# Expert weights loaded ahead into four buffers of split weights, and the pair of experts with two blocks worked on as ninth of sixteen

## The chip, the cores and the metric

The kernel runs on one core of a Trainium2 chip. The metric is the device time of one execution, in microseconds (us); of several runs the median counts. PE is the matrix engine (TensorE), DVE the vector engine, ACT the scalar engine, POOL the general engine (GpSimd), SP the engine that here does nothing but issue transfers (DMAs).

## The reference

Two blocks follow one another on 512 tokens of width 1024: first four mixers with a gate and a dense feed-forward, then a depth of two layers, each with a mixer and a mixture of experts (MoE). The change is in the MoE, which is computed like this, cut to what matters:

```python
def hierarchical_moe(h, ...):          # 4 groups x 8 experts, top 2 of the chosen group
    g = argmax(xf @ w_group + b_group)
    vals, loc = top_k((xf @ w_expert + b_expert)[group g], 2)
    gates = pg * softmax(vals); eid = g * 8 + loc
    # tokens are gathered into blocks, each of one expert
    def expert_block(args):
        xb, e = args
        hb = silu(xb @ w_gate[e]) * (xb @ w_up[e])      # 1024 -> 512
        return hb @ w_down[e]                           # 512 -> 1024
    # weighted by the gate and added up for each token
```

An expert has three float32 matrices of 2 MiB. All 32 are loaded in each layer: 201 MB.

## The kernel before

**Pairs and blocks.** `moe` takes the experts two at a time, in 16 pairs. A block is 128 rows of tokens: the first rows belong to one expert of the pair, the others to its partner. Experts are ranked by their number of tokens, and pair u joins rank u with rank 31 - u; the four experts of pairs 0 and 1 are fixed (`STAT`), so their weights can be loaded before the ranks are known. A pair of rank 2 (`NST`) up to 2 + `MORE`, which is pair 2 alone, has a second block with rows of its heavier expert only, so that more than one block's worth of its tokens finds room. `work` lists the blocks of each pair, `flat` all blocks in order; `fetch` gathers the rows of a block by an indirect transfer on POOL's queue, two blocks ahead.

**Order of the work.** The loop over `u` in `moe` runs `gate_up` of a pair, the transposes of the next pair's rows (`next_x`), then `down` and the scatter of the pair before. In `gate_up` a step `get()` takes two pieces, one for each expert of the pair, and multiplies them with every block of the pair; `down` does likewise. A pair so takes 12 pieces: four of gate, four of up, four of down. `items_moe` writes the pieces down in that order, with each pair's down behind the next pair's gate and up: piece 0 to 7 are gate and up of pair 0, 8 to 15 of pair 1, 16 to 19 the down of pair 0, 20 to 27 gate and up of the third pair, and so on to 191.

**The stream of weights.** `Stream` hands out all weights of the kernel in the order of use. It has a ring of raw buffers (`rs`, tiles `sr`, 8 KiB in each of 128 partitions) and a ring of buffers for weights that are split into a high and a low part (`hs`, tiles `sh`, each with a half `h` and a half `l` of 4 KiB). The dense stages and the mixers use the split weights; the experts read the raw ones. During an expert stage the raw ring has 13 buffers (3 + 2 from the start, 7 and 1 added for the stage) and the split ring, which has four, is not used. `prefetch` at the head of `moe` loads pieces 0 to 12 into the ring and two more into the tiles `eys` and `lngb`, which are needed for other things only later. `raw_get` then issues further loads as far ahead as there are ring buffers: a load waits on SP's queue until PE has read the piece that its buffer held. A tile named `sr_7` appears as `sr` in the trace.

```python
            r = pool.tile([P, 2048], F32, name=tag)[:, :k * c].rearrange("p (k c) -> p k c", k=k)
            self.e.Q.dma_start(r, src() if callable(src) else src)
...
        st.prefetch([(sp, "eys"), (gb, "lngb")], e.moe_first[l])
...
            self.load(max(self.nr + n, self.nr + len(self.rs) + len(self.ahead)))
```

The matmul before the stage is the mixer's output product in `token_mm` (tile `pz`), whose last rows use all four split buffers up to its end. Between it and the experts lie the layer norm, the routing on DVE (tables `eid`, `tix`) and the first gathers (`xg`). SP reads the ranked experts' numbers into registers in `ranked` (line 2334).

Of the kernel before, what the change touches and what calls it, by code (L numbers as in the profile page):

```python
# [8 lines left out]
F32 = mybir.dt.float32  # L9
# [8 lines left out]
P = 128  # L18
# [16 lines left out]
NP = NE // 2  # L35
DE = 512
ALPHA = 4.0 ** 0.25
CAP = 128
FAR = 1000.0
STAT = ((0, 8), (1, 9))  # L40
NST = len(STAT)
WIDE = 8
MORE = 1
NB = (NP + MORE + 1) // 2 * 2
CT = 32
GPC = ((640, 448, 640, 384, 448), (832, 832, 512, 320))
# [85 lines left out]
class Stream:  # L132
# [46 lines left out]

    def load(self, n, slot=None):  # L180
        while self.nl < min(n, len(self.items) if self.last is None else self.last):
            src, k, c, _, _ = self.items[self.nl]
            self.cut(self.nl, 0)
            if slot is None:
                pool, tag = self.rs[0]
                self.rs.rotate(-1)
            else:
                pool, tag = slot
                self.ahead.add(self.nl)
            r = pool.tile([P, 2048], F32, name=tag)[:, :k * c].rearrange("p (k c) -> p k c", k=k)  # L190
            self.e.Q.dma_start(r, src() if callable(src) else src)
            self.raw[self.nl] = r
            self.nl += 1

    def split(self, n):
# [50 lines left out]
    def get(self):  # L246
        n = self.i + len(self.hs)
        self.split(n if self.limit is None else max(self.i + 1, min(n, self.limit)))
        self.i += 1
        return self.hl.pop(self.i - 1)  # L250
# [1368 lines left out]
def lru(e):  # L1619
# [159 lines left out]
    for j in range(0, KT, 2):  # L1779
        for n in (1, 2, 0):  # L1780
            st.cols(w_in, n * D + j * P)
    e.mark2 = items_token(e, I["sc_w_out_2"][0], KT)
    items_moe(e, 1)
    with tc.tile_pool(name="lo", bufs=1, reuse_waits="tile") as op:
        left = mix_ln(e, op, state["z"], [slice(0, 2)] + [slice(2 + t * P, 2 + (t + 1) * P) for t in range(NT)],
# [30 lines left out]
def expert_items(weight):  # L1816


    def half(i, k, c):
        def src(q):  # L1820
            return lambda: weight(i).rearrange("(p k) c -> p k c", p=P)[:, q * k:(q + 1) * k, :]
        return [(src(q), k, c, "k", 0) for q in range(2)]
    return half(0, 4, DE) + half(1, 4, DE) + half(2, 2, D)


def chosen(e, l, ev):

    rows = (D, D, DE)
    w = [e.I[n][l].rearrange("x k c -> (x k) c") for n in MOE_W]
    return lambda i: w[i][bass.ds(ev() * rows[i], rows[i]), :]  # L1830


def items_moe(e, l):


    def own(x):
        return lambda i: e.I[MOE_W[i]][l][x]

    def ranked(r):
        return chosen(e, l, lambda: e.ranked(r))  # L1840

    e.moe_first[l] = len(e.st.items)
    last = []
    for u in range(NP):
        pair = [own(x) for x in STAT[u]] if u < NST else [ranked(u), ranked(NE - 1 - u)]
        it = [p_ for pp in zip(*(expert_items(w) for w in pair)) for p_ in pp]
        n = len(it) * 2 // 3
        for i in it[:n] + last:
            e.st.add(*i)
        last = it[n:]  # L1850
    for i in last:
        e.st.add(*i)
# [72 lines left out]
class Moe:  # L1925
# [90 lines left out]
    def run(self):  # L2016
        moe(self.e, self)
        self.ctx.close()


def moe(e, mo):
    l, hm, nt, n_tok, dh, dy, lg = mo.l, mo.hm, mo.nt, mo.n_tok, mo.dh, mo.dy, mo.lg
    nc, tc, I, st = e.nc, e.tc, e.I, e.st
# [7 lines left out]
    gb = gbp.__enter__()  # L2031
    with ExitStack() as ph:
        sp = ph.enter_context(tc.tile_pool(name=f"mo{l}", bufs=1, reuse_waits="tile"))
        st.prefetch([(sp, "eys"), (gb, "lngb")], e.moe_first[l])
        xg = [sp.tile([P, D], F32, name=f"xg{i}") for i in range(2)]
        for x_ in xg:
            G.memset(x_, 0.0)
        def small(name, shape, dt=F32):
            return sp.tile([P] + list(shape), dt, name=name)
# [54 lines left out]
        q, r = small("cq", [2, nt]), small("cr", [2, nt])  # L2094
        so4 = big(2 * nt * NE).rearrange("p (k t c) -> p k t c", k=2, t=nt)
        for o, src in ((q, pr3[:, :nt].unsqueeze(1)), (r, rank.unsqueeze(1).unsqueeze(1))):
            V.tensor_tensor(so4, sel, src.to_broadcast([P, 2, nt, NE]), op=OP.mult)
            V.tensor_reduce(o, so4, axis=AX.X, op=OP.add)
        h, u_, w, x_, z, m1 = [small(f"c{i}", [2, nt]) for i in range(6)]
# [4 lines left out]
        stt(w, u_, float(NST + WIDE), x_, OP.is_lt, OP.mult)  # L2104
        stt(x_, r, float(NST + MORE), x_, OP.is_lt, OP.mult)
        rk = small("rk", [2, nt])
# [21 lines left out]

        sv = small("sv", [2, nt, NB], F32R)
        vk = mo.val.rearrange("p t k -> p k t")  # L2130
        V.tensor_tensor(so4[:, :, :, :NB], mo.io[:, :NB].unsqueeze(1).unsqueeze(1).to_broadcast([P, 2, nt, NB]),
                        u_.unsqueeze(3).to_broadcast([P, 2, nt, NB]), op=OP.is_equal)
        mul(sv, so4[:, :, :, :NB], vk.unsqueeze(3).to_broadcast([P, 2, nt, NB]))

        def one_hots(slot_):

            for k in range(2):
                ro = sp.tile([P, KT, P], F32R, name="ext", bufs=2)
                ro = ro[:, :nt, :]
                V.tensor_tensor(ro, slot_.unsqueeze(1).to_broadcast([P, nt, P]),  # L2140
                                rk[:, k, :].unsqueeze(2).to_broadcast([P, nt, P]), op=OP.is_equal)
                yield from ((k, i, ro[:, i, :]) for i in range(nt))

        ptab = bank("ptab")[:, :NB]
        for i_, (k, t, ro) in enumerate(one_hots(mo.slot)):
            mm(ptab, ro, sv[:, k, t, :], i_ == 0, i_ == 2 * nt - 1)
        yix = small("yix", [NB], I32)
        V.tensor_scalar(yix, ptab, -1.0, None, op0=OP.add)
# [9 lines left out]
        def xpose(i):  # L2158
            x_ = sp.tile([P, KT, P], F32, name="ext", bufs=2)
            for k0 in (0, 4):  # L2160
                pt = bank("pex")
                for k in range(4):
                    tr(pt[:, k * P:(k + 1) * P], xg[i].rearrange("p (c k) -> p k c", k=KT)[:, k0 + k, :])
                (A.copy if k0 else V.tensor_copy)(x_[:, k0:k0 + 4, :].rearrange("p k c -> p (k c)"), pt)  # L2164
            return x_
# [3 lines left out]
        def tiled(o, x_, ww, cut, start, stop):  # L2169

            for c in range(0, P, CT) if cut < P else (0,):
                w_ = CT if cut < P else P
                mm(o[c:c + w_, :], x_[:, c:c + w_], ww[c >= cut], start, stop)

        def gate_up(blocks, get):

            pp = [[bank("peg") for _ in blocks] for _ in range(2)]
            for w in range(2):
                for q in range(2):
                    ww = get()  # L2180
                    for p_, (x_, cut) in zip(pp[w], blocks):
                        for k in range(4):
                            tiled(p_, x_[:, q * 4 + k, :], [i[:, k, :] for i in ww], cut, q + k == 0, q == 1 and k == 3)
            res = []
            for (_, cut), pg, pu in zip(blocks, *pp):
                sg = sp.tile([P, DE], F32, name="eh", bufs=3)
                A.activation(sg, pg, AF.Silu)  # L2187
                mul(sg, sg, pu)
                res.append((sg, cut))
            return res  # L2190
# [9 lines left out]
        def down(blocks, get):  # L2200
            pp = [[bank("pey0"), bank("pey1")] for _ in blocks]
            for q in range(2):
                ww = get()
                for po, (h_, cut) in zip(pp, blocks):
                    for k in range(2):
                        for h in range(2):
                            tiled(po[h], h_[:, q * 2 + k, :], [w[:, k, h * 512:h * 512 + 512] for w in ww], cut,
                                  q + k == 0, q + k == 2)
            return pp

# [11 lines left out]
        def gates():  # L2222
# [28 lines left out]
            stt(b2, bs, float(NST + WIDE), b1, OP.is_lt, OP.mult)  # L2251
            stt(b1, rank, float(NST + MORE), b1, OP.is_lt, OP.mult)
            ts(bs, rank, float(NP), -2.0, OP.is_ge, OP.mult)
# [55 lines left out]
        lst = small("lst", [NL + 1], I32)  # L2309
        nov = small("nov", [1], I32)  # L2310

        work = [[u] + ([NP + u - NST] if NST <= u < NST + MORE else []) for u in range(NP)]
        flat = [b_ for bs in work for b_ in bs]

        def fetch(i):
            if i < len(flat):
                gather(i % 2, tix[:, flat[i]:flat[i] + 1])
# [23 lines left out]
        def next_x(u):  # L2341

            xs = []
            for b_ in work[u]:
                i = done[0]
                done[0] += 1
                xs.append((xpose(i % 2), P if b_ >= NP else CAP * 3 // 4 if NST <= u < NST + WIDE else CAP // 2))
                fetch(i + 2)
            return xs

        xs = next_x(0)
        gates()
        st.nr = e.moe_first[l]
# [7 lines left out]
        for u in range(NP):  # L2361
            sg = gate_up(xs, get)
            if u + 1 < NP:
                xs = next_x(u + 1)
# [5 lines left out]
            if u == NP - 2:  # L2370
                next(rows)
            hs = [(hpose(x_), cut) for x_, cut in sg]
        scatters(NP - 1, down(hs, get))
        with tc.issue_after(e.late.ins):
            for h, n in rows_:
# [109 lines left out]
```

## Time and profile before

| | us |
|---|---|
| median of 3 runs | 2599.82 (2596.87 to 2601.62) |
| the profiled execution | 2602.1 |
| its span, first to last instruction | 2600.1 |
| PE busy | 2309.3 (89%) |
| DVE busy | 939.5 (36%) |
| ACT busy | 667.3 (26%) |
| POOL busy | 239.3 (9%) |
| expert matmuls of gate and up, busy (PE L286, `peg`) | 534.5 |
| expert matmuls of down, busy (PE L286, `pey`) | 309.8 |
| mean granted TensorE clock | 0.958 |

The span of a profile begins with the first instruction; the profiled execution's own time is 2.0 us longer. Times in the rows below are us from the start of the span, times of single instructions in the page's groups are ns. "Busy" adds up the time in which at least one instruction of the group runs; the expert matmuls run four at a time beside each other. Line 286 is a helper that issues every matmul, line 191 the one that issues every load of weights, so groups are told apart by their tiles. The layer numbers are 0 and 1; layer 0's expert stage runs from about 1290 to 1778, layer 1's from about 2062 to 2550.

### The profile page before, as it was taken

The page shows a single profiled execution, that of the slowest core. Times are in us where ns is not written, and L with a number is a line of the kernel's source. Part 1 is how long each engine was busy: PE and PEld are TensorE (multiplying, and loading weights), DVE is VectorE, ACT ScalarE, POOL GpSimd, SP SyncE. Part 2 cuts the span into 40 slices and gives each one's busy share as a digit, 9 for nine tenths or more (in the row PEclk, how much of TensorE's full clock was granted, in tenths as well). Part 3 has the DMA queues.
Part 4 walks back from the last instruction along what each step waited for, and adds up shares of the span by engine and source line. Part 5 has one row for each costly group of instructions (what it writes and reads, how often), then busy time and mean ns, then how long its engine had stood idle before and what let it go on. Part 6 is the DMA issues. An engine that isn't in the chain of part 4 may idle for free. (4 is left out here: it accounts for less than half of the span.)

```text
span 2600.1 us, 37405 instructions
## 1 busy us (share of the span) xinstructions
PE 2309.3 (89%) x15293; PEld 1479.3 (57%) x15293; DVE 939.5 (36%) x2127; ACT 667.3 (26%) x1062; POOL 239.3 (9%) x268
## 2 busy tenths in 40 slices
PE   7998999999999999999699888883999699888881
PEld 6886778887888888896433222221997433222220
DVE  4348877754533322665510000004544410000003
ACT  4335332123422222584201000004322101000002
POOL 0013130000100000101200000002101110000002
PEclk9999999999999999999699999996999699999996
DMA  4221221035133333224299999996236299999993
GB/s 140 90 84 37 86 69 62 22 98 182 58 97 97 97 115 113 76 75 185 99 407 416 420 419 415 412 418 245 68 98 236 114 403 418 418 419 413 414 407 123
DMA packets 175218, 556.85 MB, mean 214 GB/s; under 512 B 22088, under 2 KB 104742, under 8 KB 124866
## 3 DMA queue, kind: packets, MB, share of 16 engines
q1 hardware_dynamic: 153156, 523.29, 52.0%
q0 software_dynamic: 12768, 25.31, 2.7%
q10 hardware_dynamic: 9120, 5.83, 0.8%
q8 instruction: 122, 2.00, 0.3%
q14 instruction: 52, 0.43, 0.0%
HBM read 548.00 MB, written 25.21 MB: 220 GB/s over the span
## 5 line engine op out<-in xcount | busy, mean ns | idle before, releaser
L286 PE MATMUL peg<-sr,ext 128*32 128x512 f32 (+1 forms) x4096 | 534.5, 595 | 90.8 <-DMA sr<-in_moe_w_gate_dram 55.4
L286 PEld LDWEIGHTS peg<-sr,ext 128*32 128x32 f32 (+1 forms) x4096 | 143.5, 110 | 426.6 <-issue 261.0
L286 PE MATMUL pey<-sr,eh 128*32 128x512 f32 (+1 forms) x2080 | 309.8, 597 | 13.9 <-DMA sr<-in_moe_w_down_dram 11.3
L286 PEld LDWEIGHTS pey<-sr,eh 128*32 128x32 f32 (+1 forms) x2080 | 84.5, 110 | 200.0 <-issue 154.2
L2164 DVE COPY ext<-pex 128x512 f32<-128x512 f32 x34 | 23.5, 690 | 407.7 <-PE pex L305 407.5
L213 DVE TENSOR_TENSOR sh_0l<-sr,sh_0h 128x1024 fp32r<-128x1024 f32 x84 | 103.5, 1232 | 162.2 <-ACT sh_0h L211 161.5
L2218 ACT COPY eys<-pey 128x512 f32<-128x512 f32 x68 | 39.9, 586 | 456.2 <-PE pey L286 455.6
L271 DVE TENSOR_TENSOR eh<-eh,peg 128x512 f32<-128x512 f32 x34 | 23.4, 688 | 349.8 <-PE peg L286 349.8
L211 ACT CAST sh_0h<-sr 128x1024 fp32r<-128x1024 f32 x84 | 88.1, 1049 | 235.9 <-PE pf L286 53.2
L213 DVE TENSOR_TENSOR sh_1l<-sr,sh_1h 128x1024 fp32r<-128x1024 f32 (+1 forms) x65 | 77.4, 1191 | 111.6 <-ACT sh_1h L211 111.3
L213 DVE TENSOR_TENSOR sh_2l<-sr,sh_2h 128x1024 fp32r<-128x1024 f32 (+1 forms) x65 | 74.4, 1144 | 95.5 <-ACT sh_2h L211 95.1
L211 ACT CAST sh_1h<-sr 128x1024 fp32r<-128x1024 f32 (+1 forms) x65 | 66.5, 1023 | 153.1 <-PE pf L286 48.5
L211 ACT CAST sh_2h<-sr 128x1024 fp32r<-128x1024 f32 (+1 forms) x65 | 62.9, 967 | 152.6 <-PE pf L286 49.3
L2187 ACT ACTIVATE eh<-peg 128x512 f32<-128x512 f32 x34 | 20.3, 597 | 288.7 <-PE peg L286 288.7
L286 PE MATMUL pl<-hlo,sh_0h 128*128 128x264 f32 (+3 forms) x288 | 87.6, 304 | 2.0 <-DVE hlo L295 2.0
L286 PE MATMUL pl<-hhi,sh_0h 128*128 128x264 f32 (+3 forms) x288 | 88.0, 305 | 0.8 <-ACT hhi L294 0.8
L2219 POOL DMA_INDIRECT dy<-eys,yix x34 | 33.8, 993 | 583.8 <-ACT eys L2218 567.4
L286 PE MATMUL pl<-hhi,sh_0l 128*128 128x264 f32 (+3 forms) x288 | 87.2, 303 | 0.0
L2154 POOL DMA_INDIRECT xg<-dh,tix x34 | 34.9, 1028 | 360.2 <-PE pex L305 299.1
L2197 DVE COPY eh<-pex 128x512 f32<-128x512 f32 x34 | 23.3, 691 | 111.8 <-PE pex L305 111.8
L2164 ACT COPY ext<-pex 128x512 f32<-128x512 f32 x34 | 19.9, 586 | 154.9 <-PE pex L305 115.9
L286 PEld LDWEIGHTS pl<-hlo,sh_0h 128*128 128x128 f32 x288 | 56.4, 196 | 4.5 <-DVE hlo L295 2.7
(714 smaller groups left out, 4881.2 us busy)
## 6 DMA issues: line engine op xcount, KB each, us to landing
sr<-in_moe_w_gate_dram SPq DMA_DIRECT2D x128, 1024.0 KB
sr<-in_moe_w_down_dram SPq DMA_DIRECT2D x128, 1024.0 KB
sr<-in_moe_w_up_dram SPq DMA_DIRECT2D x124, 1024.0 KB
sr<-in_w_in_dram SPq DMA_DIRECT2D x34, 1024.0 KB
sr<-in_sc_w_in_dram SPq DMA_DIRECT2D x12, 1024.0 KB
sr<-in_ffn_w_gate_dram SPq DMA_DIRECT2D x11, 1024.0 KB
sr<-in_ffn_w_up_dram SPq DMA_DIRECT2D x11, 1024.0 KB
sr<-in_ffn_w_down_dram SPq DMA_DIRECT2D x10, 1024.0 KB
```

The lines of the kernel that those rows point to most:

```text
L211: self.e.A.copy(hi, r)
L213: v.tensor_tensor(lo, r, f(hi), op=OP.subtract)
L271: V.tensor_tensor(out_, a, b, op=OP.mult)
L286: T.matmul(o, l, r, start=start, stop=stop)
L2154: G.indirect_dma_start(out=xg[i], out_offset=None, in_=dh[:, :], in_offset=bass.IndirectOffsetOnAxis(ap=ti, axis=0), bounds_check=n_tok - ...
L2164: (A.copy if k0 else V.tensor_copy)(x_[:, k0:k0 + 4, :].rearrange("p k c -> p (k c)"), pt)
L2187: A.activation(sg, pg, AF.Silu)
L2197: V.tensor_copy(hh.rearrange("p k c -> p (k c)"), pt)
L2218: e.late = A.copy(ys[:, h * 512:(h + 1) * 512], po[h])
L2219: G.indirect_dma_start(out=dy[:, :], out_offset=bass.IndirectOffsetOnAxis(ap=yi, axis=0), in_=ys, in_offset=None, bounds_check=2 * n_tok - ...
```

## The change

`prefetch` is also given the four split buffers (`*st.hs`), so that four more pieces (15 to 18) are loaded ahead. A split buffer is two tiles of half a piece, so such a piece comes in two transfers; a raw piece is therefore kept as a list of its 128-partition slices, and `gate_up` and `down` index that list. `ORDER` takes pair 2 out of its place and puts it in the middle: 0, 1, 3, 4, 5, 6, 7, 8, 2, 9, ..., 15. `items_moe` (the order of the loads) and `work` (that of the blocks) follow it. The number of rows of the first expert in a block (`cut`) is now chosen by the block and not by the place of the pair.

```diff
+ORDER = [u for u in range(NP) if not NST <= u < NST + MORE]
+ORDER[NP // 2:NP // 2] = range(NST, NST + MORE)
...
     def load(self, n, slot=None):
...
-            r = pool.tile([P, 2048], F32, name=tag)[:, :k * c].rearrange("p (k c) -> p k c", k=k)
-            self.e.Q.dma_start(r, src() if callable(src) else src)
-            self.raw[self.nl] = r
+            src = src() if callable(src) else src
+            if (pool, tag) in self.hs:
+
+                rr = [pool.tile([P, 1024], F32, name=tag + x).rearrange("p (k c) -> p k c", c=c) for x in "hl"]
+                for i, r in enumerate(rr):
+                    self.e.Q.dma_start(r, src[:, i * k // 2:(i + 1) * k // 2, :])
+            else:
+                rr = [pool.tile([P, 2048], F32, name=tag)[:, :k * c].rearrange("p (k c) -> p k c", k=k)]
+                self.e.Q.dma_start(rr[0], src)
+
+            self.raw[self.nl] = rr[0] if parts else [r[:, i, :] for r in rr for i in range(r.shape[1])]
...
-    for u in range(NP):
+    for u in ORDER:
         pair = [own(x) for x in STAT[u]] if u < NST else [ranked(u), ranked(NE - 1 - u)]
...
-        st.prefetch([(sp, "eys"), (gb, "lngb")], e.moe_first[l])
+        st.prefetch([(sp, "eys"), (gb, "lngb"), *st.hs], e.moe_first[l])
...
-                            tiled(p_, x_[:, q * 4 + k, :], [i[:, k, :] for i in ww], cut, q + k == 0, q == 1 and k == 3)
+                            tiled(p_, x_[:, q * 4 + k, :], [i[k] for i in ww], cut, q + k == 0, q == 1 and k == 3)
...
-                            tiled(po[h], h_[:, q * 2 + k, :], [w[:, k, h * 512:h * 512 + 512] for w in ww], cut,
+                            tiled(po[h], h_[:, q * 2 + k, :], [w[k][:, h * 512:h * 512 + 512] for w in ww], cut,
...
-        work = [[u] + ([NP + u - NST] if NST <= u < NST + MORE else []) for u in range(NP)]
+        work = [[u] + ([NP + u - NST] if NST <= u < NST + MORE else []) for u in ORDER]
...
-                xs.append((xpose(i % 2), P if b_ >= NP else CAP * 3 // 4 if NST <= u < NST + WIDE else CAP // 2))
+                xs.append((xpose(i % 2), P if b_ >= NP else CAP * 3 // 4 if NST <= b_ < NST + WIDE else CAP // 2))
```

## Rows read from the trace of the kernel before

**Rows 1.** The page, the span in 40 slices of 65 us: what the transfers moved.

```profile
GB/s 140 90 84 37 86 69 62 22 98 182 58 97 97 97 115 113 76 75 185 99 407 416 420 419 415 412 418 245 68 98 236 114 403 418 418 419 413 414 407 123
```

**Rows 2.** Waits of PE, 1280 to 1780: us in total, times, longest.

```profile
PE peg L286 <- DMA sr<-in_moe_w_gate_dram: 28.0, 18, 1.8
PE peg L286 <- DMA sr<-in_moe_w_up_dram: 17.5, 20, 1.5
...
PE pey L286 <- DMA sr<-in_moe_w_down_dram: 5.7, 11, 0.6
```

**Rows 3.** Windows of 20 us, layer 0: busy by engine, clock, DMA share, GB/s.

```profile
1240.00:1260.00 20.00, 17.34 (x113) 15.94 (x112) 9.50 (x24) 6.14 (x13) 8.32 (x8) 0.71 0.50 195
1260.00:1280.00 20.00, 5.66 (x28) 4.96 (x26) 14.88 (x78) 4.07 (x7) 1.95 (x4) 0.50 0.07 27
...
1300.00:1320.00 20.00, 20.00 (x186) 7.00 (x182) 1.98 (x3) 1.78 (x3) 1.00 (x1) 1.00 1.01 421
...
1340.00:1360.00 20.00, 20.00 (x117) 6.59 (x110) 0.69 (x1) 1.20 (x2) 0.00 (x0) 1.00 1.00 410
1360.00:1380.00 20.00, 20.00 (x176) 7.36 (x178) 2.58 (x4) 2.36 (x4) 2.05 (x2) 1.00 0.97 379
```

**Rows 4.** Timeline of SP's queue, layer 0: start, us, what it issues.

```profile
1240.79 0.42 SPq L191 DMA_DIRECT2D eys<-in_moe_w_up_dram  x1
1297.25 0.33 SPq L191 DMA_DIRECT2D sr<-in_moe_w_up_dram  x1
...
1492.38 7.96 SPq L191 DMA_DIRECT2D sr<-in_moe_w_gate_dram  x4
...
1524.66 7.97 SPq L191 DMA_DIRECT2D sr<-in_moe_w_gate_dram  x4
```

**Rows 5.** Timeline of PE, layer 0: start, us, matmuls merged by tile.

```profile
1240.22 0.40 PE L286 MATMUL pz<-sh_0h,zl 128*128 128x512 f32 x1
...
1332.64 28.88 PE L286 MATMUL peg<-sr,ext 128*32 128x512 f32 x160
...
1362.32 7.07 PE L286 MATMUL pey<-sr,eh 128*32 128x512 f32 x64
...
1370.48 13.94 PE L286 MATMUL peg<-sr,ext 128*32 128x512 f32 x128
...
1385.45 14.47 PE L286 MATMUL pey<-sr,eh 128*32 128x512 f32 x80
```

**Rows 6.** Timeline of POOL, and SP's longest single wait, layer 0.

```profile
1285.39 1.12 POOL L2154 DMA_INDIRECT xg<-dh,tix  x1 [23.45 <-DVE tix L2150]
...
1333.00 1.03 POOL L2219 DMA_INDIRECT dy<-eys,yix  x1 [5.67 <-ACT eys L2218]
...
SPq L2334 <- DVE eid L2329: 44.7, 1, 44.7
```

**Rows 7.** A window of 3 us at the first release of a buffer, layer 0.

```profile
1296.00:1299.00 3.00, 3.00 (x32) 0.91 (x28) 0.00 (x0) 0.00 (x0) 0.00 (x0) 1.00 0.32 52
```

**Rows 8.** Timeline of SP's queue, single issues behind the first pair's down.

```profile
1332.06 0.33 SPq L191 DMA_DIRECT2D sr<-in_moe_w_down_dram  x1
...
1339.94 0.34 SPq L191 DMA_DIRECT2D sr<-in_moe_w_gate_dram  x1
```

**Rows 9.** Layer 1: SP's first load after the start, POOL's first gather.

```profile
2068.74 0.33 SPq L191 DMA_DIRECT2D sr<-in_moe_w_up_dram  x1
...
2056.06 1.10 POOL L2154 DMA_INDIRECT xg<-dh,tix  x1 [28.74 <-DVE tix L2150]
```

**Rows 10.** Timelines of ACT (end of two pairs' gate, last copy) and PE (first wait).

```profile
1407.49 0.60 ACT L2187 ACTIVATE eh<-peg 128x512 f32<-128x512 f32 x1 [6.89 <-PE peg L286]
1432.92 0.60 ACT L2187 ACTIVATE eh<-peg 128x512 f32<-128x512 f32 x1 [6.23 <-PE peg L286]
...
1777.50 0.59 ACT L2218 COPY eys<-pey 128x512 f32<-128x512 f32 x1 [0.28 <-PEq L2379]
...
1446.35 2.76 PE L286 MATMUL pey<-sr,eh 128*32 128x512 f32 x18 [0.20 <-DMA sr<-in_moe_w_down_dram]
```

More of the change, by code (lines that the diff above doesn't have):

```diff
@@ L181, in load @@
         while self.nl < min(n, len(self.items) if self.last is None else self.last):
-            src, k, c, _, _ = self.items[self.nl]
+            src, k, c, _, parts = self.items[self.nl]
             self.cut(self.nl, 0)
```

## The prediction

> **What bounds the kernel now.** I read the page's 40 slices first [rows 1]. They show two stretches, slices 21 to 27 and 33 to 39, in which the transfers run at 400 to 420 GB/s: the two expert stages, one for each layer. Everything the change touches lies in them and in the slices just ahead. Next I asked whom PE waits for in layer 0's stage [rows 2]: 28.0 + 17.5 + 5.7 = 51 us, all of it for expert weights. So the stage's end is set by the last weights to land, and PE has slack. The third view, windows of 20 us, says when [rows 3]: from 1300 on the transfers are at 421 GB/s, but for a dip in 1340 to 1380, with 410 and 379. Ahead of the stage they are nearly idle: 27 GB/s in 1260 to 1280. That idle time is what the change can use.
>
> The SP queue shows why it is idle [rows 4]: the last load ahead goes out at 1240.8, and the next at 1297.25, when PE has used up its first two pieces. In between no buffer is free in the plan: 13 ring buffers and two borrowed ones (`eys`, `lngb`) hold pieces 0 to 14. Layer 1 does the same 771.5 us later [rows 9].
>
> **Four more pieces.** A piece is 1.049 MB (1024 KB); at 418.5 GB/s, between the slices' 412 to 420 [rows 1] and the window's 421 [rows 3], it takes 2.506 us. In steady state one pair of experts (12 pieces, with its gathers and scatters) takes 32.28 us, from the gate loads at 1492.38 to those at 1524.66 [rows 4]. Pieces 15 to 18 now go into the four buffers of split weights. The last matmul that reads those is at 1240.22 [rows 5], so their loads go out right behind the two borrowed ones, some 1241 to 1250. The transfers already queued end about 1250 (3.9 MB went in 1240 to 1260 [rows 3]); four pieces end about 1260. The first gather, which needs the transfers, is issued at 1285.39 [rows 6]: 25 us of cover in layer 0, and in layer 1 about 2030 against 2056.06 [rows 9]. If that cover were gone, the 10 us would stand in front of the gather and be lost again. What is left to load from 1297 on is 173 pieces in place of 177: **-4 x 2.506 = -10.0 us per layer**.
>
> The rate can be questioned. The slices give 412 to 420 GB/s over hundreds of us [rows 1], so 2.506 us it is. The Trainium skill ("HBM Reference", Specifications) puts a core's share of its memory at about 358 GB/s, and about 425 for a core that streams alone; by the share, which no window here agrees with, eight pieces would cost 23.4 us instead of 20.1, and the time would be an estimated 2576.8.
>
> The eight half loads cost SP eight issues of 0.42 us at most [rows 4], 3 us in all. Behind them SP has only the register loads of line 2334, for which it waits 44.7 us for `eid` [rows 6]; they are hidden by that, and a release as late as 1280 would still be. The larger number of views of a piece in `gate_up` and `down` issues nothing, and the cut of a block goes by its own number, so each block has its old instructions.
>
> **The queue at the hand-over.** The borrowed buffers are used once, so piece 32 must wait for the ring slot of piece 19. Pieces 19 to 31 take the slots of 0 to 12, which came free at the times of the trace. The load issued at 1297.25 moves bytes from about 1298.7 on: the window 1296 to 1299 has 52 GB/s [rows 7], which is 156 KB or 0.4 us at the full rate. So 1.4 us pass from issue to bytes. Thirteen pieces end at 1298.7 + 13 x 2.506 = 1331.3. Piece 19 is used up with the second half of the first pair's down, whose release the SP queue has at 1332.06 [rows 8]; 32 flows from 1333.5: 2.2 us empty. It ends at 1336.0. Pieces 33 and 34 wait for the first quarter of the third pair's gate and up, which with one block takes 13.94 / 4 = 3.5 us from 1332.64 on [rows 5]: out at 1336.1, flowing at 1337.5: 1.5 us empty. After that two slots come free per 3.5 us and two pieces take 5.0, so the queue fills up. Sum 3.7 us, less a scatter (0.52 MB, 1.25 us) that is issued at 1333.00 [rows 6] and has to be moved anyway: **+2.45 us** (bounds 0, if gathers fill it, and 3.7).
>
> **The pair with two blocks, moved.** Pair 2 holds two blocks: its gate and up take 28.88 us against 13.94 of the next pair, its down 14.47 against 7.07 [rows 5]; with transposes it is some 24 us longer. As third pair it holds slots while the loads could run: quarters of 7.2 us, and the queue runs empty, which is the dip of 1340 to 1380: (8.5 + 39.5) x 20 / 418.5 = 2.3 us. With the old order and four more pieces, slots come free at 1339.94 [rows 8] and every 28.88 / 4 = 7.2 us after it, and the same counting (a slot's release + 1.4 us, less the end of what is queued) gives empty times of 2.2 + 5.3 + 2.2 + 2.3 + 2.2 = 14 us: the pieces would be worth nothing. At the ninth place the queue can't run empty: PE, which does an ordinary pair in 25.4 us (the activations at 1407.49 and 1432.92 [rows 10]) against 32.28 of the loads, has by then used up its lead. In the pair's 49.4 us the loads gain 17.1 us, 6.4 pieces of the ring's 13, and some five are still to be loaded. **-2.3 us.** The 24 us by which PE then lags come back at 32.28 - 25.4 = 6.9 us a pair, in 3.5 pairs; seven follow. POOL's gathers keep their places in the row of blocks, two ahead; their number is the same.
>
> **Sum.** Per layer -10.0 + 2.45 - 2.3 = -9.8 us (bounds -12.3 and -8.6, by the bounds of the empty time); two layers -19.7 us (-24.6 to -17.2). The profiled execution took 2602.1 us (span 2600.1), the median of three runs is 2599.8; the two lie 0.1% apart. 2602.1 - 19.7 = 2582.4 for a profiled one, **2580.1** from the median. Nothing in the later stages changes: they shift. A measurement of this kernel can tell about 0.2%, 5 us, from no change.
>
> **Rivals.**
> *The hand-over costs more.* If the queue stood empty for 1.5 us at each of the third pair's four quarters and not at one, 8.2 us are lost at the hand-over and the gain is 10.0 + 2.3 - 8.2 = 4.1 us per layer: 2592. For it: in this stretch PE's releases, not the rate, set when loads go out. Against: two slots per 3.5 us are more than the rate can use.
> *The pieces don't go out early* (another wait keeps the loads in SP's queue until PE starts). Then all of the four pieces' time stays, only the dips go or stay: 2597 to 2600. Against: the last reader of the buffers is done at 1240.6 [rows 5], and the load ahead of them in the queue went out right then [rows 4].
> *The moved pair stops the loads amid the stage.* If at the ninth place the ring is full of landed pieces, its 49.4 us of PE against 32.28 of loads stop the queue for 17.1 us per layer: -9.8 + 17.1 = +7.3, twice: **2615**, slower. It decides when PE's lag at that place exceeds some five pieces. For it: the dip of the old third place is this very stop, small because the queue was still full. Against: PE waits for weights from 1446 on [rows 10], after which the lead is nil, and without the pair it will be nil earlier.
> *More than the bounds*, below 2575: the first stretch holds some cost that I don't see and that falls away.
>
> **Numbers.** Forecast 0.69 (its own range 2575 to 2583, with 2.5 us for the spread of runs on either side), dearer hand-over 0.12, not early 0.07, stopped amid 0.08, more 0.04. Faster 0.85, same 0.07, slower 0.08. The range 2573 to 2593 holds the forecast with its spread and the dearer hand-over, about 0.81.
>
> **What would show it.** Right: over 390 GB/s in 1240 to 1260 and about nothing in 1262 to 1284; PE's first expert matmul unchanged near 1290.9, in layer 1 some 10 us earlier; the first load after the start still near 1297; a short dip at 1331 to 1338 and none at 1360; PE's waits for weights beginning near 1390 in place of 1446, absent in the double pair and for three pairs behind it, and back at the end; the last output copy of layer 0 near 1767.7 in place of 1777.50 [rows 10], and in layer 1 twice as much earlier. Wrong: a load into a split buffer later than 1280, a first gather later than 1286, or a window below 350 GB/s behind the double pair.

## The result, and the profile after

| | before | after |
|---|---|---|
| median, four runs of each on one chip | 2598.65 us (2596.87 to 2601.62) | 2576.35 us (2574.67 to 2578.68) |
| ratio, 95% interval | | 0.9913 [0.99, 0.9925] |
| profiled execution, span | 2602.1, 2600.1 | 2577.2, 2575.1 |
| PE's waits for expert weights, layer 0's stage | 51 [rows 2] | 40.5 |
| first load after the start to last copy, layer 0 | 1297.25 to 1777.50 = 480.25 [rows 4, 10] | 1292.94 to 1763.35 = 470.41 |
| the same, layer 1 | 2068.74 to 2549.90 = 481.16 | 2054.22 to 2525.20 = 470.98 |

The two expert stages are 9.84 and 10.18 us shorter, 20.0 together; 19.7 was forecast. The profiled spans differ by 25.0. Of the other 5.0, 0.7 lie between the layers and behind layer 1; 4.3 lie ahead of the first load: 2.6 us stand there at the last `pz` already (1240.22 [rows 5], 1237.61 after), and most of the rest in the routing, where 16 `plg` matmuls took 3.47 us in the trace of before and 1.94 in this one; the granted clock was 0.50 there before (1250 to 1254) and 1.00 here (1247 to 1250). A second profile of the changed kernel (run 4 below) takes 50.5 us from the last `pz` to the first expert matmul, against 50.7 before and 48.5 here, and has its first expert activation at 1299.40, against 1300.75 before and 1296.44 here. So this part belongs to the single execution and not to the change.

The page after, its span, its engines and the transfers in 40 slices, answers to [rows 1]: the two stretches at 405 to 420 GB/s are there, and each is followed sooner by its end.

```profile
span 2575.1 us, 37407 instructions
PE 2305.2 (90%) x15293; PEld 1475.1 (57%) x15293; DVE 939.0 (36%) x2127; ACT 666.8 (26%) x1062; POOL 238.5 (9%) x268
GB/s 141 91 79 43 87 70 63 22 99 168 69 88 98 98 131 99 91 69 196 152 370 420 420 414 416 412 418 263 69 83 239 160 411 419 418 414 414 414 405 120
```

SP's queue after, to be held against [rows 4 and 9] (line numbers are 11 higher; L198 issues the half loads, L201 the whole ones). The half loads go out from 1233.62 on, one by one as the split buffers come free, some of them ahead of `eys`. The first load into the ring follows at 1292.94, 53 us behind `eys`; before it was 56.5.

```profile
1233.62 0.33 SPq L198 DMA_DIRECT2D sh_0l<-in_moe_w_up_dram  x1
1234.04 0.38 SPq L198 DMA_DIRECT2D sh_0h<-in_moe_w_up_dram  x1
...
1239.91 0.54 SPq L201 DMA_DIRECT2D eys<-in_moe_w_up_dram  x1
...
1241.36 0.33 SPq L198 DMA_DIRECT2D sh_0l<-in_moe_w_down_dram  x1
1292.94 0.33 SPq L201 DMA_DIRECT2D sr<-in_moe_w_down_dram  x1
```

POOL's first gather answers to [rows 6]. It comes 21 us behind the end of the early transfers, so their cover held. In layer 1 they end near 2015, and the first gather goes out at 2041.39.

```profile
1280.65 1.12 POOL L2165 DMA_INDIRECT xg<-dh,tix  x1 [23.35 <-DVE tix L2161]
```

Windows of 20 us of after, layer 0; columns as in [rows 3], the last one GB/s:

```profile
1240.00:1260.00 20.00, 19.09 (x122) 17.85 (x122) 9.11 (x22) 5.44 (x12) 9.02 (x9) 0.70 0.89 355
1260.00:1280.00 20.00, 3.24 (x18) 2.89 (x17) 18.33 (x84) 3.48 (x6) 0.00 (x0) 0.50 0.00 0
1300.00:1320.00 20.00, 20.00 (x182) 7.48 (x178) 3.08 (x5) 1.27 (x3) 1.55 (x2) 1.00 1.02 422
1320.00:1340.00 20.00, 20.00 (x188) 6.26 (x184) 0.88 (x2) 2.27 (x4) 2.62 (x3) 1.00 0.98 387
1340.00:1360.00 20.00, 20.00 (x187) 6.71 (x183) 1.98 (x3) 2.36 (x4) 2.07 (x2) 1.00 1.01 418
1360.00:1380.00 20.00, 20.00 (x183) 6.82 (x178) 1.98 (x3) 1.84 (x4) 2.03 (x2) 1.00 1.01 420
1500.00:1520.00 20.00, 20.00 (x107) 5.51 (x105) 0.00 (x0) 1.20 (x2) 0.99 (x1) 1.00 1.01 419
1520.00:1540.00 20.00, 20.00 (x136) 7.84 (x138) 2.94 (x5) 1.76 (x3) 1.75 (x2) 1.00 1.00 404
1580.00:1600.00 20.00, 20.00 (x167) 7.17 (x165) 2.07 (x3) 2.36 (x4) 2.43 (x3) 1.00 1.02 410
1600.00:1620.00 20.00, 16.68 (x132) 5.58 (x123) 1.38 (x2) 1.18 (x2) 1.64 (x2) 1.00 1.01 409
```

The dip of 1340 to 1380 [rows 3] is gone. In its place stand a short one at the hand-over (387 in 1320 to 1340, (418.5 - 387) x 20 / 418.5 = 1.5 us) and a smaller one in the double pair (404 in 1520 to 1540, 0.7 us). Layer 1 has 395 and 402 in the like windows, 1.1 and 0.8 us.

Whom PE waits for in 1280 to 1780 after, to be held against [rows 2], total, times and longest in us: the first wait starts earlier (1386 in place of 1446 [rows 10]), and the sum is 10.7 us less.

```profile
PE peg L297 <- DMA sr<-in_moe_w_gate_dram: 19.7, 13, 1.8
PE peg L297 <- DMA sr<-in_moe_w_up_dram: 14.7, 16, 1.6
PE pey L297 <- DMA sr<-in_moe_w_down_dram: 6.1, 11, 0.9
```

### The profile page after: what moved, and what is told of

The parts are those of the page before. It is cut to its first block, busy times and chain, and to the rows that moved or that the text cites. A ratio compares the mean times of both kernels' runs of the same rounds, so it can differ in the third digit from the quotient of the medians.

```text
span 2575.1 us, 37407 instructions
## 1 busy us (share of the span) xinstructions
PE 2305.2 (90%) x15293; PEld 1475.1 (57%) x15293; DVE 939.0 (36%) x2127; ACT 666.8 (26%) x1062; POOL 238.5 (9%) x268
## 5 line engine op out<-in xcount | busy, mean ns | idle before, releaser
L297 PE MATMUL peg<-sr,ext 128*32 128x512 f32 (+1 forms) x4064 | 527.0, 596 | 70.0 <-DMA sr<-in_moe_w_gate_dram 39.1
L297 PE MATMUL pey<-sr,eh 128*32 128x512 f32 x1984 | 303.2, 597 | 14.9 <-DMA sr<-in_moe_w_down_dram 12.4
L297 PEld LDWEIGHTS pey<-sr,eh 128*32 128x32 f32 x1984 | 82.1, 110 | 194.8 <-issue 149.5
L222 ACT CAST sh_1h<-sr 128x1024 fp32r<-128x1024 f32 (+1 forms) x65 | 66.5, 1023 | 146.7 <-PE pf L297 48.5
L297 PEld LDWEIGHTS pl<-hhi,sh_0h 128*128 128x128 f32 x288 | 55.2, 192 | 4.7 <-ACT hhi L305 2.5
```

Source lines behind the costliest of these rows:

```text
L222: self.e.A.copy(hi, r)
L297: T.matmul(o, l, r, start=start, stop=stop)
```

## The experiments

Theory: the four pieces save their time on the transfers in each layer, but only if no other place in the stage lets the queue of loads run empty; the moved pair sees to that. Rivals: each part works alone and the two add up; the old place was the main loss; the moved pair is late enough to cost something of its own. "Stage" below is the time from the first expert activation to the last copy of the layer, which leaves the stretch ahead of it out: 476.75 and 477.66 us before, 466.91 and 467.48 after.

**1. The move alone.**

```diff
-        st.prefetch([(sp, "eys"), (gb, "lngb"), *st.hs], e.moe_first[l])
+        st.prefetch([(sp, "eys"), (gb, "lngb")], e.moe_first[l])
```

> The order of the change without the four pieces. Theory (each layer is over when its last weights have landed; the empty queue at the double pair costs 2.3 us per layer): about 4.6 us faster than before in all, ratio 0.998; in the trace no dip of the transfers at 1360 to 1380, and PE's first wait for weights earlier than 1446. Rival (the moved pair stops the loads amid the stage): slower than before by up to 2 x 17 us, with a window below 350 GB/s behind the double pair. Rival (the move has a value of its own on PE): faster by more than 8 us.

2598.40 us against 2597.84 in the medians, ratio 0.999 [0.9981, 0.9999]: the times hardly tell it from before. Stage 476.01 and 477.03, 0.7 us a layer less; three profiles of the changed kernel differ by 0.2 us in layer 0 and 0.7 in layer 1, so this too is near the spread. The windows say why it is not 2.3:

```profile
1340.00:1360.00 20.00, 20.00 (x188) 6.74 (x180) 1.98 (x3) 1.75 (x3) 2.06 (x2) 1.00 1.01 419
1360.00:1380.00 20.00, 18.93 (x153) 6.01 (x146) 2.07 (x3) 1.18 (x2) 1.03 (x1) 1.00 1.02 420
1540.00:1560.00 20.00, 20.00 (x161) 7.76 (x158) 3.26 (x5) 1.92 (x4) 2.02 (x2) 1.00 0.99 399
```

The old dip is filled, but part of it comes back as a new one where the pair now stands. The moved pair does not stop the loads amid the stage: no window of 20 us in or behind it is below 394 GB/s in either layer until the loads end.

**2. The pieces alone, with the old order.**

```diff
-ORDER = [u for u in range(NP) if not NST <= u < NST + MORE]
-ORDER[NP // 2:NP // 2] = range(NST, NST + MORE)
+ORDER = list(range(NP))
```

> The four pieces without the move: pair 2 stays the third. Theory: the pieces save 10.0 us per layer and the queue then stands empty for some 14 us per layer in place of 2.3, so between 4 us slower and 2 us faster than before in all, ratio 0.9993 to 1.0015; windows far below 418 GB/s between 1330 and 1365. Rival (the pieces count whatever the order): 20 us faster, ratio 0.992.

2598.04 us, ratio 1.0 [0.9991, 1.001]; stage 476.91 and 477.62, as before.

```profile
1320.00:1340.00 20.00, 20.00 (x153) 7.20 (x152) 2.10 (x4) 2.57 (x5) 3.75 (x5) 1.00 0.81 311
1340.00:1360.00 20.00, 20.00 (x112) 7.47 (x114) 1.97 (x3) 1.55 (x3) 1.04 (x1) 1.00 0.77 284
1360.00:1380.00 20.00, 20.00 (x188) 6.52 (x180) 1.29 (x2) 1.77 (x3) 1.01 (x1) 1.00 0.99 401
```

The missing bytes are worth (107.5 + 134.5 + 17.5) x 20 / 418.5 = 12.4 us; before's dip was 2.3. The loads reach the early double pair 10 us sooner and stand still in it for 10 us longer. So neither part is worth much by itself (0.7 and 0), and together they are worth 10 a layer: the parts do not add up, which rules that rival out. It also rules out that the old place was the main loss by itself.

**3. Two of the four pieces.**

```diff
-        st.prefetch([..., *st.hs], e.moe_first[l])
+        st.prefetch([..., *list(st.hs)[:2]], e.moe_first[l])
```

> The change with two of the four split buffers. Theory: a piece loaded ahead is worth 2.506 us per layer, so half of the pieces' 20 us stay, and the hand-over dip is smaller or gone: 13 to 15 us faster than before, ratio 0.9945 to 0.995. Rival (the hand-over dip eats a good part of the last two pieces): as fast as the whole change within 4 us, ratio 0.9925 or less.

2586.91 us, ratio 0.9955 [0.9941, 0.9969], 10.9 us below before where 13 to 15 were expected; stage 471.10 and 471.76, 5.7 and 5.9 below before. Against the move alone that is 4.9 and 5.3 us for two pieces, and the other two bring 4.2 and 4.3 more: 2.1 to 2.6 us a piece, against 2.506 of the transfer. The first two cause no dip at the hand-over, 419 GB/s in its window:

```profile
1320.00:1340.00 20.00, 20.00 (x184) 6.79 (x180) 1.98 (x3) 2.35 (x4) 3.17 (x4) 1.00 1.02 419
```

**4. The changed kernel again**, unedited.

> The changed kernel once more, on the same chip as the three others. Theory: 20 to 22 us faster than before, ratio 0.9915 to 0.9925; 9.8 to 10.2 us of it in each layer between the first release of a buffer and the last output copy. What is more than 20 us lies ahead of layer 0's stage and is chance of the run: it should not come back in the same place.

2578.98 us, ratio 0.9917 [0.9904, 0.9931]; stage 466.96 and 467.09.

**5. The double pair as sixth.**

```diff
-ORDER[NP // 2:NP // 2] = range(NST, NST + MORE)
+ORDER[5:5] = range(NST, NST + MORE)
```

> The change with the double pair as sixth of sixteen. Theory: PE's lead is used up near 1386, within the fifth pair, so the double pair stops nothing there either: as the change within 2 us, ratio 0.9915 to 0.9925. Rival (the place amid the stage matters as such, or the ring is still full there): dips below 380 GB/s behind the pair and 5 us or more slower than the change.

2579.08 us, ratio 0.9932 [0.9918, 0.9946], a little above what was expected; stage 466.44 and 467.05, the change's within half a us.

**6. The double pair as fourteenth**, by the same edit with 13.

> The change with the double pair as fourteenth; two pairs follow. Theory: in the pair PE falls 49.4 - 32.3 = 17.1 us behind the loads, two pairs give back 2 x 6.9 = 13.8: about 3.3 us per layer are left at the end, 6 to 7 us slower than the change, ratio 0.994 to 0.995. Rival (the stage ends with the last landing wherever the pair stands): as the change, ratio 0.992.

2598.47 us, ratio 1.0003 [0.9994, 1.0012]; stage 478.36 and 478.18: 11.4 and 10.7 us above the change, three times what was expected. The windows of the pair behind the double one and PE's instructions there show a second cost. Columns of the windows as in [rows 3]; the third number from the end is the granted clock:

```profile
1735.00:1740.00 5.00, 5.00 (x13) 2.06 (x12) 0.00 (x0) 2.40 (x6) 0.97 (x1) 0.97 0.80 303
1740.00:1745.00 5.00, 5.00 (x18) 1.41 (x21) 0.69 (x1) 1.17 (x2) 0.41 (x1) 0.50 0.85 356
1745.00:1750.00 5.00, 5.00 (x44) 1.35 (x40) 0.00 (x0) 0.00 (x0) 0.56 (x1) 0.84 0.39 130
```

```profile
1737.08 4.59 PE L297 MATMUL pgb<-lngb,row 2*128 2x512 f32 x8
...
1742.66 15.86 PE L297 MATMUL peg<-sr,ext 128*32 128x512 f32 x128
```

The eight `pgb` matmuls are the last norm's gain and bias, spread over all partitions from two rows. Before and after they ran as two fours, 5.5 us apart, at full clock. These are the lines of after:

```profile
1713.20 1.98 PE L297 MATMUL pgb<-lngb,row 2*128 2x512 f32 x4
1715.11 3.63 PE L297 MATMUL pey<-sr,eh 128*32 128x512 f32 x24
1718.67 1.98 PE L297 MATMUL pgb<-lngb,row 2*128 2x512 f32 x4
```

Here they run in one go, behind the double pair's down, and amid them the granted clock falls to 0.50, the 1.2 GHz level. By the three windows it stays there for 0.3 + 5.0 + 1.6 = some 6.9 us. Layer 1 has the same fall, with 0.62 and 0.70 in 2510 to 2520.

**7. The double pair as last**, the same edit with 15.

> The change with the double pair last. Theory: PE's 17 to 24 us behind the loads come back nowhere: 34 to 48 us slower than the change, 12 to 26 us slower than before, ratio 1.005 to 1.010. Rival: as the change, ratio 0.992.

2627.72 us, ratio 1.0109 [1.0094, 1.0125]; stage 22 us a layer above the change, 488.99 and 490.16. The whole is 48.7 us above run 4, just over the 34 to 48 that were expected. The rival of the slower side exists, then, but at a later place than the change's: behind the last pair no load is left to hide its extra work, and 22 of the 24 us that the prediction gave it show.

**8. Fourteenth again, with the `pgb` work at an earlier pair.**

```diff
-            if u == NP - 2:
+            if u == NP // 2:
                 next(rows)
```

> The double pair as fourteenth once more, with the second step of the layer norm's gain and bias (eight matmuls of two rows, tile pgb) moved from the last pair but one to the ninth pair. Theory (of the 12 us per layer that this place costs, 4.6 are these matmuls, which stood on a PE that was behind, and some 3 the lower clock granted right behind them): 4 to 5 us per layer stay, 8 to 10 us slower than the change, ratio 0.995 to 0.996, and no window with a clock under 1.00 between 1735 and 1755. Rival (the lag is the double pair's alone): as at that place before, ratio 1.000.

2586.77 us, ratio 0.9958 [0.9944, 0.9971]; stage 471.87 and 471.30, and the clock holds:

```profile
1735.00:1740.00 5.00, 5.00 (x22) 2.00 (x24) 0.37 (x1) 2.34 (x4) 0.97 (x1) 1.00 0.79 323
1740.00:1745.00 5.00, 5.00 (x52) 1.53 (x48) 0.32 (x1) 0.00 (x0) 0.00 (x0) 1.00 1.00 381
1745.00:1750.00 5.00, 5.00 (x52) 1.57 (x48) 0.00 (x0) 0.60 (x1) 0.98 (x1) 1.00 0.97 364
```

So of the 11 us of the fourteenth place some 4.4 (5.0 and 3.8) are lag that two pairs cannot take up, and 6.7 (6.5 and 6.9) hang on those eight matmuls standing where they do. How much of the 6.7 is the fall of the clock and how much the matmuls' own time (4.59 us) was not measured apart; 6.9 us at half the clock are at most an estimated 3.5.

**9. The split buffers as part of the ring for the whole stage**, so that their four pieces are not used once but over and over, and the hand-over goes away.

```diff
-        st.prefetch([(sp, "eys"), (gb, "lngb"), *st.hs], e.moe_first[l])
+        st.cuts.append([e.moe_first[l] + 12 * NP, list(st.hs), None])
+        st.rs.extend(st.hs)
+        st.prefetch([(sp, "eys"), (gb, "lngb")], e.moe_first[l])
```

> The change with the four split buffers kept in the ring during the stage, so that they are loaded again (ring of 17 in place of 13 and four used once). Theory: the hand-over dip (about 1.5 us per layer in the change's trace) goes, as do the smaller ones: 2 to 5 us faster than the change, ratio 0.9905 to 0.9915, and no window of 3 us below 400 GB/s between 1320 and 1340. Rival (the dip is no cost, since gathers fill it): as the change within 1 us.

2586.51 us, ratio 0.9955 [0.9941, 0.9968]: some 8 us worse than the change, where it should have been better; stage 471.02 and 473.97, 4.1 and 6.5 above it. The hand-over is indeed whole (418 in 1320 to 1340), but when the half loads come round, the rate falls, here and in like stretches (342 in 1464 to 1468):

```profile
1320.00:1340.00 20.00, 20.00 (x184) 6.78 (x180) 1.98 (x3) 2.27 (x4) 3.14 (x4) 1.00 1.02 418
1500.00:1504.00 4.00, 3.42 (x27) 0.83 (x28) 0.00 (x0) 0.00 (x0) 0.00 (x0) 1.00 1.01 410
1504.00:1508.00 4.00, 4.00 (x22) 1.35 (x15) 0.00 (x0) 1.17 (x2) 0.60 (x1) 1.00 1.02 398
1508.00:1512.00 4.00, 4.00 (x29) 1.12 (x28) 0.00 (x0) 0.00 (x0) 0.40 (x1) 1.00 0.93 345
1512.00:1516.00 4.00, 4.00 (x26) 0.97 (x26) 0.00 (x0) 0.00 (x0) 0.00 (x0) 1.00 0.99 358
1516.00:1520.00 4.00, 4.00 (x22) 1.51 (x15) 0.00 (x0) 0.60 (x1) 0.00 (x0) 1.00 1.03 411
```

The DMA share stays at 0.93 to 1.03 meanwhile. That does not tell an empty queue from slower transfers: in the hand-over dip of after, 1332 to 1336, 337 GB/s stand beside a share of 0.98. Two separate tiles are not enough for it, for ahead of the stage the half loads of after go into the same tiles, with whole loads among them, at full rate:

```profile
1248.00:1252.00 4.00, 3.45 (x26) 3.06 (x25) 0.82 (x2) 1.80 (x3) 0.80 (x1) 0.94 1.05 427
```

**10. Every piece as two half loads** into its usual buffer, to see whether the halves by themselves do that.

```diff
-                self.e.Q.dma_start(rr[0], src)
+                if parts:
+                    self.e.Q.dma_start(rr[0], src)
+                else:
+                    for i in range(2):
+                        z = slice(i * k // 2, (i + 1) * k // 2)
+                        self.e.Q.dma_start(rr[0][:, z, :], src[:, z, :])
```

> The change with every piece of expert weights loaded in two transfers of half a piece, into the same buffers. Theory (a half load costs more than half of a whole one: the kernel with the split buffers in the ring lost some 6 to 8 us per layer, beside what it should have gained, over about 81 half loads, 0.07 to 0.1 us each): the other 173 pieces become 346 half loads, 24 to 35 us per layer, 48 to 70 us slower than the change, ratio 1.010 to 1.018. Rival (it was the two separate tiles or the order of the ring): as the change, ratio 0.992.

2593.37 us, ratio 0.998 [0.9971, 0.9989], 15 us above the change and less than expected. In 1400 to 1500 the transfers of after and of this kernel:

```profile
DMA packets 6493, 41.99 MB, mean 420 GB/s; under 512 B 1128, under 2 KB 1128, under 8 KB 1617
```

```profile
DMA packets 11495, 40.26 MB, mean 403 GB/s; under 512 B 1684, under 2 KB 1684, under 8 KB 11488
```

Packets of half the size cost 4% of the rate in this window; over 1300 to 1740 it is 404 against 415 GB/s, 2.7%, and the stage is 474.67 and 476.24, 7.8 and 8.8 us above the change. That is far from the 345 to 358 of the run above: what else slows the mixture of whole and half loads amid the stage stays open.

**11. The early pieces written further down**, behind the read of a rank, to have them go out late.

```diff
-        st.prefetch([(sp, "eys"), (gb, "lngb"), *st.hs], e.moe_first[l])
+        st.prefetch([(sp, "eys"), (gb, "lngb")], e.moe_first[l])
...
+        ranked(3)
+        for slot in list(st.hs):
+            st.load(st.nl + 1, slot)
```

> The change with the loads into the split buffers held on SP's queue until the experts' ranks are known, some 40 us later, so that they start just ahead of the first expert matmul. Theory (what counts is only that they move in idle time): the queue is idle from then until the first release, about 8 of their 10 us per layer, so 2 to 5 us slower than the change, ratio 0.992 to 0.994, and the first gathers land later by at most a few us. Rival (loads beside the gathers put the whole 10 us in front of the stage): 15 us or more slower than the change, ratio 0.998 or more.

2578.95 us, ratio 0.9926 [0.9913, 0.994]. The edit did not do what it was for: in SP's queue the half loads still go out at 1233.86 to 1241.68, so they were not held back.

```profile
1233.86 0.33 SPq L198 DMA_DIRECT2D sh_0l<-in_moe_w_up_dram  x1
...
1241.68 0.63 SPq L198 DMA_DIRECT2D sh_0l<-in_moe_w_down_dram  x1
```

So this is a repeat of the changed kernel, and what late loads would cost was not tried further. No version beat the change.

## Why the prediction was right, and where its steps were not

The forecast of 2580.1 lies 3.7 us above the measured 2576.35; the repeats gave 2578.98 and 2578.95. In the two stages 20.0 us were gained where 19.7 were forecast; the closeness is partly luck, since two terms of the sum were wrong and cancel.

**Four pieces, -10.0 us a layer: right.** The stages became 9.8 and 10.2 us shorter, and two pieces bring 4.2 to 5.3 us (run 3) where two transfers take 5.0. The loads went out earlier than forecast, from 1233.62 and not from 1241, because the split buffers come free one at a time. That is why 1240 to 1260 shows 355 GB/s and not over 390: a part had moved already (373 GB/s in 1236 to 1240, 120 before). Nothing in 1260 to 1280 and the gather at 1280.65 show the cover intact. By the Trainium skill's share of 358 GB/s ("HBM Reference", Specifications) the estimate was 2576.8, nearer to this median than the forecast and farther from both repeats; the windows of after stand at 408 to 422 GB/s outside the dips, so that is chance and no case for the share.

**The hand-over, +2.45: the right kind, a little too dear.** 1.5 and 1.1 us were lost, inside the bounds of 0 to 3.7. The activations behind it come every 22.65 us:

```profile
1334.61 0.60 ACT L2198 ACTIVATE eh<-peg 128x512 f32<-128x512 f32 x1 [7.12 <-PE peg L297]
1357.26 0.60 ACT L2198 ACTIVATE eh<-peg 128x512 f32<-128x512 f32 x1 [7.09 <-PE peg L297]
```

The dearer hand-over (8.2 us) did not happen.

**The moved pair, -2.3: this step failed as it was put.** "At the ninth place the queue can't run empty" does not hold: 404 and 402 GB/s stand in the double pair, and from 1500 to 1545 SP's loads wait 10.8 us for PE to free a buffer, against 1.3 from 1440 to 1485. The move alone is worth some 0.7 us a layer, since the dip follows the pair in part. The sum still came out because two errors cancel: +2.45 - 2.3 = +0.15 was forecast, and 1.5 + 0.7 us (layer 1: 1.1 + 0.8) of new dips stand against 2.3 of the old one, -0.1 and -0.4. What the move is really worth is in run 2: without it the pieces are worth nothing, with 12.4 us of empty queue where 14 had been counted.

**The lag behind the double pair: right in size, over a pair sooner than forecast.** Right behind the hand-over an ordinary pair takes PE 22.65 us and not 25.4. Amid the stage the forecast's pace holds: from the activation at 1580.45 to that at 1606.81 PE takes 26.36 us, of which it waits 1.04, so 25.3; layer 1 gives 25.3 too. The slack is 32.28 - 25.3 = 7.0 us a pair, as forecast (6.9). PE's gate and up of the double pair and of the pairs behind it:

```profile
1498.51 31.92 PE L297 MATMUL peg<-sr,ext 128*32 128x512 f32 x156
...
1539.41 7.92 PE L297 MATMUL peg<-sr,ext 128*32 128x512 f32 x70
...
1573.29 7.92 PE L297 MATMUL peg<-sr,ext 128*32 128x512 f32 x68
...
1603.14 4.41 PE L297 MATMUL peg<-sr,ext 128*32 128x512 f32 x32 [1.04 <-DMA sr<-in_moe_w_gate_dram]
```

From 1498.51 to 1573.29 are 74.8 us, 24.2 more than two ordinary pairs (the forecast had 24) and 10.2 more than two pairs of loads. The next pair, to 1598.15, gives 7.4 back. PE's waits are absent in the double pair and for two pairs behind it; three were forecast. The fourteenth place prices the lag: two pairs behind the double one left 3.3 us by the forecast and 4.4 were measured with the clock intact.

The double pair's gate and up take 31.92 us there, against 28.88 at the third place [rows 5], with no wait in the rows. The loads are not shown to cause this: the same time stands at the sixth place (run 5, first line) and with half loads at 403 GB/s (run 10, second line).

```profile
1400.71 31.92 PE L297 MATMUL peg<-sr,ext 128*32 128x512 f32 x156
```

```profile
1501.04 31.95 PE L301 MATMUL peg<-sr,ext 128*32 128x512 f32 x157
```

What differs in the trace is the order. At the third place PE takes, piece by piece, all matmuls of the first block and then those of the second; at the ninth the two blocks come by turns in smaller groups. What that order costs was not tried.

**Where the place starts to cost.** The rival of the slower side needed a place too late, not a full ring amid the stage: sixth and ninth cost the same, fourteenth 4.4 us a layer more with the clock intact, and last 22. The places between ninth and fourteenth were not tried.

## What to carry to other kernels

Time taken off a bound resource counts only if nothing behind it stops that resource again: before filling an idle stretch, look for the next place where the queue can run empty, and try the parts alone and together. A piece of extra work for an engine with slack belongs where enough ordinary steps follow to take up the lag (here extra time over slack per step, 24 / 7.0, some three and a half), and early enough that the last transfers still hide it. A short burst of unusual work that was harmless while its engine had slack can turn costly where the engine is late.

## What the runs showed of the hardware

Loads of 0.5 MB moved at 403 GB/s where those of 1 MB moved at 420, in the same queue and into the same buffers (1400 to 1500; 404 against 415 over 1300 to 1740). Whole loads mixed with halves into two separate tiles moved at 345 to 358 GB/s for stretches of some 8 us, with the DMA engines shown busy at 0.93 or more; why stays open.

Eight matmuls with two rows each, 4.59 us in the middle of a busy PE, saw the granted clock fall to 0.50 for some 6.9 us, in both layers; as two fours 5.5 us apart they ran at 1.00. The pair behind them took 15.86 us for gate and up, in place of 13.94 in run 8. They are not the only thing that goes before a fall: runs 9 and 10 have windows of 20 us at 0.91 without them (1480 to 1500 and 1460 to 1480).
